# Half-wise transposes placed among matmuls, and a recurrence tail in two parts, in a two-block layer stack of split-precision matmuls

## The chip, the cores and the metric

The kernel runs on one core of one Trainium2 chip. Its time is device microseconds (us) of one execution of the whole program, the median of several runs. Engines are named as in the profile: PE is TensorE (matmuls), PEld its weight loads, DVE is VectorE, ACT is ScalarE, POOL is GpSimd, SP is SyncE, which issues nearly all DMA loads here.

## The reference, cut to what matters

There are 256 tokens of width 1024. The first block has two layers. Each normalises `x`, projects it and runs three branches: a gated MLP (a), latent attention (b) and a gated linear recurrence (c). They are projected, gated and summed:

```
h = rmsnorm(x, pre_norm_g[l]);  proj = h @ w_in[l]
y_a = gmlp_spatial(u, v, ...) * silu(z_a)
y_b = mla_attention(...)      * silu(z_b)
y_c = rg_lru(x_c, ...)        * silu(z_c)
merged = (sigmoid(g_a) * (y_a @ w_proj_a[l]) + sigmoid(g_b) * (y_b @ w_proj_b[l])
          + sigmoid(g_c) * (y_c @ w_proj_c[l]))
x = x + rmsnorm(merged @ w_out[l], post_norm_g[l])
```

`rg_lru` is a recurrence along the tokens on 1280 channels: with `a = exp(log_a)` and `b = sqrt(max(1 - a*a, 0)) * i * x`, the state is `h[t] = a[t] * h[t-1] + b[t]`. The gates `a` and `i` come from small block-diagonal products.

The second block has two layers too. Layer 0 mixes by pooling windows, layer 1 by a sparse attention (NSA). Both then do

```
x = x + conv_ffn(rmsnorm(x, norm_ffn[i]), ...)               # 1024 -> 2 x 2816 -> 1024
gate = sigmoid(rmsnorm(x, norm_ple[i]) @ ple_gate[i])
x = x + gate * (p[i] @ ple_proj[i])
```

and the attention of layer 1 starts from two norms of the `x` that this gate leaves in layer 0. A last norm gives the output. Everything is float32.

## The kernel before

**Numbers and tiles.** A float32 operand is kept as two parts of a reduced type that TensorE takes, a high part `hi` and a low part `lo`. A product is three matmuls (`mm3`, lines 481 to 483: hi by hi, hi by lo, lo by hi). The 256 tokens are two halves of 128. A token-major product has one half's features as the stationary operand and 512 weight columns moving; a feature-major one (`feat_pair`) has weights as the stationary operand and all 256 tokens moving. The results stand in PSUM tiles `psA` (four buffers) and `psB`.

**Weights.** They come in chunks of 512 KB in one fixed order (`Stream.get`, line 382). A request for a chunk first issues the loads of the next chunks (`raw_ahead`, 3) on SP's queue into four buffers `raw`, and the splits of the next ones (`split_ahead`, 2): the high part on ScalarE (L376), the low part on VectorE in two pieces of 512 columns (L379), in seven buffers `hi` and `lo`. A `raw` buffer is free again once its low part is made.

**Order.** The scheduler sets the order on each engine, from the order in which the program is written and from the data that each instruction needs. An engine then works through its own list strictly in order.

**A token-major group.** `tok_halves` asks for all four chunks of a product, then does half 0 with all of them, then half 1. `tok_group` was a list of its two results. `tok_pair` does it for two such products at once (`PAIR_HELD`, 6 of 8 chunks held).

**A norm.** `norm` returns `run(half)`. With `fold` it multiplies `x` by a row of gains (L555, tile `h`), starts the sum of squares on ScalarE (L512) and the inverse root behind it (L501, L502), and at once transposes `h` on TensorE (L538, 128 x 128 each) and splits the result into `hT` (ScalarE L488, VectorE L489; L491 and L492 where a scale is applied). The factor of the norm itself is applied later.

**The recurrence's tail** (`first_layer`, lines 975 to 1001). The merge order is `ga` 0 and `pa` 0 (the gate and the projection of branch a, first 512 columns), the recurrence's gates for its first half, `ga` 1 and `pa` 1, and the other gates (`gates`, tanh on ScalarE L967 into `tmp`, exp L973 into `av`). Then follow both groups of the merge gate `gc` with their tanh (L898) and the part that changes, in this order:

```
tg = [gate("gc", n) for n in range(2)]                                                    # L980
...
    nc.vector.tensor_tensor(tv[j], av[j], av[j], op=ALU.mult)                             # L985, five tiles
    nc.vector.tensor_scalar(tv[j], tv[j], 1.0, None, op0=ALU.min)                         # L986
    nc.scalar.activation(tv[j], tv[j], AF.Sqrt, bias=quarter, scale=-0.25)                # L987
...
    nc.vector.tensor_tensor(xc[j], xc[j], tv[j], op=ALU.mult)                             # L989, five tiles
        nc.vector.tensor_tensor_scan(ctile(av, ct), ctile(av, ct), ctile(xc, ct), 0.0, ...)   # L992, ten halves
```

Behind it the branch's own gate `zc` is computed in five feature-major pairs of tiles (240 matmuls of 256 columns). Each has a tanh (L617), a product (L618) and one with the state (L1001), and is split into `yc` (L491, L492). `pc`, the projection of `yc`, is two token-major groups of 60 matmuls. Its results are added to `merged`, which is transposed (L538) for `w_out`. In layer 1 the tile `pT` (256 KB) and a row of gains in two halves are loaded between the scans and `zc`.

**The feed-forward network** (`ffn`). It has 22 tiles of activations, and its last seven down-projections (`FFN_TAIL`) are done half 0 first, then half 1, 42 matmuls each. Behind all of them each half's sums are added to `x` (L1165) and the next norm's `run` follows. **The gate** (`ple`, lines 1182 to 1199) does the same behind `tok_pair`: for each half tanh, product and sum (L1195 to L1197), then `run`. In layer 0 this is the norm from which the attention starts; in layer 1 it is the last one, without transposes.

Of the kernel before, what the change touches and what calls it, by code (L numbers as in the profile page):

```python
# [16 lines left out]
P = 128  # L17
# [170 lines left out]
FFN_TAIL = 7  # L188
PAIR_HELD = 6
# [229 lines left out]
class Net:  # L419
# [123 lines left out]
    def norm(self, *key, dst=None, rs=None, fold=None):  # L543
# [6 lines left out]
        def run(half):  # L550
            if fold:
                hs = self.u2s("h", 2)
                for n, h in enumerate(hs):
                    cs = slice(n * 512, (n + 1) * 512)
                    self.nc.vector.tensor_tensor(h, self.x[half][:, cs], gain[n], op=ALU.mult)  # L555
            if run_rs[half] is None:
                run_rs[half] = self.rs_x(half, fold or 1.0)
            if not fold:
                hs = self.scaled_x(half, run_rs[half], gain)
            for n, h in enumerate(hs):  # L560
                self.transpose_split(h, dst, half, 4 * n, 4)

        run.dst, self.rs = dst, run_rs
# [15 lines left out]
    def tok_pair(self, key, f):  # L579

        ps = [[self.psA(), self.psA()] for _ in range(2)]
        def part(half, i, w):
            n, c = divmod(i, 4)
            for k in range(2):
                kg = 2 * c + k
                self.mm3(ps[n][half], f.pair(kg, half), (w[0][:, k, :], w[1][:, k, :]), kg == 0, kg == KD - 1)
# [146 lines left out]
    def first_layer(self, l):  # L733
# [119 lines left out]
        for n in range(2):  # L853
            ps = self.tok_group(("v", l, n), hT)
# [23 lines left out]
        for n in range(2):  # L878
            ps = self.tok_group(("u", l, n), hT)
# [4 lines left out]
        for n in range(2):  # L884
            ps = self.tok_group(("za", l, n), hT)
# [8 lines left out]
        def gate(gk, n):  # L894
            ts = []
            for ps in self.tok_halves((gk, l, n), hT):
# [4 lines left out]
        def project(pk, n, y, kts, ts, first=False):  # L901
            for half, ps in enumerate(self.tok_halves((pk, l, n), y, kts=kts)):
# [71 lines left out]

        for kind, i in MERGE_ORDER:
# [4 lines left out]
        tg = [gate("gc", n) for n in range(2)]  # L980
# [135 lines left out]
    def ffn(self, l):  # L1116
# [26 lines left out]

        def down(*js):
            ws = [self.w.get(("down", l, j), 512) for j in js]
            for half in range(2):
                sl = slice(half * P, half * P + P)
                for j, (wh, wl) in zip(js, ws):
                    f = act[j]
                    for n in range(2):  # L1150
                        self.mm3(acc[half][n], (f[:, 0, sl], f[:, 1, sl]), (wh[:, n, :], wl[:, n, :]),
                                 j == 0, j == KF - 1)
# [8 lines left out]
        down(*range(KF - FFN_TAIL, KF))  # L1161
        for half in range(2):
# [3 lines left out]
            nxt(half)  # L1166
# [8 lines left out]
    def ple_in(self, l, n):  # L1175
        if n == 0:
            self.pp = [[], []]
        ps = self.tok_group(("pp", l, n), self.pf, kts=2)
# [5 lines left out]
    def ple(self, l):  # L1184
# [5 lines left out]
        pss = self.tok_pair(("pg", l), hT)  # L1190
        for half in range(2):
            for n in range(2):
                cs = slice(n * 512, n * 512 + 512)
                t = self.tmp()
                nc.scalar.activation(t, pss[n][half], AF.Tanh, scale=rs[half])  # L1195
                nc.vector.scalar_tensor_tensor(t, t, 1.0, self.pp[half][n], op0=ALU.add, op1=ALU.mult)
                nc.vector.tensor_tensor(self.x[half][:, cs], self.x[half][:, cs], t, op=ALU.add)  # L1197
            nxt(half)
# [15 lines left out]
    def nsa(self):  # L1214
# [15 lines left out]
        ps = self.tok_group(("kv", 0), h1)  # L1230
# [72 lines left out]
        def keys_values(s):  # L1303
            ps = self.tok_group(("kv", 1 + s), h1)
# [43 lines left out]
        def queries(n):  # L1348
            ps = self.tok_group(("qb", n), hT)
# [206 lines left out]
```

## Time and profile before

| what | value |
| --- | --- |
| median of three runs | 1441.75 us (1443.41, 1441.58, 1441.75) |
| profiled execution | 1441.76 us |
| its span in the trace | 1440.0 us |
| mean granted TensorE clock | 0.994 of full speed |
| busy in the span: PE, DVE, ACT, POOL | 1399.3, 1049.4, 844.6, 92.0 us |
| DMA | 249.32 MB, mean 173 GB/s |

The span runs from the first to the last instruction on the core, and the time of an execution holds 1.76 us more around it. Busy time counts an instruction from its start to its modelled end; register work and DMA issue are not counted. PE's and PEld's times lie beside each other, so they are not added. Means over the span hide stages with different limits, and the losses spoken of below are fractions of a per cent of it.

### The profile page before, as it was taken

Reading aid. Unit: us, or ns where it says so; the run is one execution under the profiler, and the core shown is the slowest. Engines: PE = TensorE matmul, PEld = TensorE weight load, DVE = VectorE, ACT = ScalarE, POOL = GpSimd, SP = SyncE. Lnnn points to the kernel's source line nnn. Section 1 sums busy time; section 2 is a strip of 40 time slices with the busy share of each in tenths; the row PEclk is TensorE's granted clock in tenths of the full one; section 3 lists DMA queues with packets and bytes.
Section 4 is the critical chain, followed back from the end, with each engine's and each line's share of the span. In section 5 each row is a group of like instructions: output and inputs, shape, how many; then the busy total and the mean of one; then the engine's idle time right before and its main releaser. Section 6 shows DMA issues by size and latency. Waiting matters only on the chain.

```text
span 1440.0 us, 23026 instructions
## 1 busy us (share of the span) xinstructions
PE 1399.3 (97%) x8506; PEld 1236.1 (86%) x8506; DVE 1049.4 (73%) x2131; ACT 844.6 (59%) x1421; POOL 92.0 (6%) x155
## 2 busy tenths in 40 slices
PE   6999999999999999999999999999999999999997
PEld 6987889889789878898897899999888778999985
DVE  7856748659767676577687688777696788787765
ACT  6665545656455665456655466555565796665554
POOL 1000002100010000021000000000010440000000
PEclk9999999999999999999999999999999999999999
DMA  8553555564646634665656555555555115655652
GB/s 282 183 196 117 163 188 190 168 214 136 228 139 207 214 118 129 194 201 161 203 175 231 163 181 186 191 178 189 183 172 171 50 38 189 194 180 189 188 164 86
DMA packets 73408, 249.32 MB, mean 173 GB/s; under 512 B 8272, under 2 KB 8912, under 8 KB 73296
## 3 DMA queue, kind: packets, MB, share of 16 engines
q1 hardware_dynamic: 72576, 245.95, 52.1%
q10 hardware_dynamic: 720, 1.91, 0.5%
q8 instruction: 67, 1.10, 0.3%
q14 instruction: 45, 0.37, 0.1%
HBM read 246.77 MB, written 1.05 MB: 172 GB/s over the span
## 4 chain that ended last, share of the span: by engine, by line
PE 81%; DVE 9%; ACT 5%; DMA 3%; issue 2%; POOL 1%; POOLq 0%; ACTq 0%; DVEq 0%; SPq 0%
PE psA L481 22%; PE psA L483 22%; PE psA L482 22%; PE psB L481 3%; DVE lo L379 3%; PE psB L482 3%; DMA raw<-in_w_dram 3%; PE psB L483 3%; ACT hi L376 2%; PE psB L538 1%; ACT es L1415 1%; DVE av L992 1%; POOL rs L502 1%; PE psB L1054 1%; PE psB L1036 1%
## 5 line engine op out<-in xcount | busy, mean ns | idle before, releaser
L379 DVE TENSOR_TENSOR lo<-raw,hi 128x512 fp32r<-128x512 f32 (+2 forms) x897 | 585.0, 679 | 221.3 <-ACT hi L376 215.8
L376 ACT ACTIVATE hi<-raw 128x1024 fp32r<-128x1024 f32 (+3 forms) x449 | 467.6, 1045 | 309.8 <-PE psA L483 112.3
L482 PE MATMUL psA<-hT,hi 128*128 128x256 f32 x1160 | 328.6, 283 | 0.5 <-DVE hT L489 0.5
L483 PE MATMUL psA<-hT,lo 128*128 128x256 f32 x1160 | 328.2, 283 | 0.0
L481 PE MATMUL psA<-hT,hi 128*128 128x256 f32 x1160 | 328.1, 283 | 0.0
L481 PE MATMUL psA<-hi,hT 128*128 128x512 f32 (+2 forms) x592 | 230.6, 390 | 3.2 <-ACT hT L488 3.2
L482 PE MATMUL psA<-lo,hT 128*128 128x512 f32 (+2 forms) x592 | 228.5, 386 | 1.4 <-DVE lo L379 1.4
L483 PE MATMUL psA<-hi,hT 128*128 128x512 f32 (+2 forms) x592 | 229.1, 388 | 0.0
L482 PEld LDWEIGHTS psA<-hT,hi 128*128 128x128 f32 x1160 | 221.9, 191 | 2.0 <-DVE hT L489 0.7
L481 PEld LDWEIGHTS psA<-hT,hi 128*128 128x128 f32 x1160 | 221.8, 191 | 1.6 <-ACT hT L488 0.2
L483 PEld LDWEIGHTS psA<-hT,lo 128*128 128x128 f32 x1160 | 221.9, 191 | 0.0
L481 PEld LDWEIGHTS psA<-hi,hT 128*128 128x128 f32 x592 | 111.8, 189 | 22.6 <-ACT hT L488 4.1
L482 PEld LDWEIGHTS psA<-lo,hT 128*128 128x128 f32 x592 | 111.5, 188 | 21.4 <-DVE lo L379 2.1
L483 PEld LDWEIGHTS psA<-hi,hT 128*128 128x128 f32 x592 | 111.5, 188 | 20.4 <-DVE hT L489 0.5
L502 POOL TENSOR_TENSOR rs<-ms,mhalf 128x1 f32<-128x1 f32 x34 | 28.3, 832 | 977.1 <-DVE ms L501 788.1
L1135 DVE SCALAR_TENSOR_TENSOR tmp<-psA,colt,tmp 128x255 f32<-128x255 f32 (+1 forms) x176 | 84.2, 478 | 1.2
L481 PE MATMUL psB<-hi,fact 128*128 128x512 f32 x176 | 68.8, 391 | 0.0
L482 PE MATMUL psB<-lo,fact 128*128 128x512 f32 x176 | 68.8, 391 | 0.0
L483 PE MATMUL psB<-hi,fact 128*128 128x512 f32 x176 | 68.5, 389 | 0.0
L1132 ACT ACTIVATE tmp<-psA,colt 128x256 f32<-128x256 f32 x88 | 48.5, 551 | 1.9
L936 POOL CAST es<-xs 64x256 fp32r<-64x256 f32 x48 | 29.4, 640 | 270.1 <-ACT xs L488 269.3
L512 ACT ACTIVATE junk<-x 128x512 bf16<-128x512 f32 x36 | 22.6, 629 | 36.8 <-DVE x L1165 14.0
(342 smaller groups left out, 2238.1 us busy)
## 6 DMA issues: line engine op xcount, KB each, us to landing
raw<-in_w_dram SPq DMA_DIRECT2D x414, 512.0 KB, 3.6
raw<-in_w_dram SPq DMA_DIRECT2D x24, 384.0 KB, 3.8
row<-in_rows_dram SPq DMA_DIRECT2D x34, 256.0 KB, 5.4
raw<-in_w_dram SPq DMA_DIRECT2D x8, 448.0 KB, 3.2
raw<-in_w_dram SPq DMA_DIRECT2D x4, 480.0 KB, 3.3
x<-in_x_dram SPq DMA_DIRECT2D x4, 256.0 KB, 4.3
pm<-in_pm_dram ACTq DMA_DIRECT2D x2, 512.0 KB, 5.2
out_dram<-h SPq DMA_DIRECT2D x4, 256.0 KB, 2.1
```

What stands on the lines that cost most here:

```text
L376: self.nc.scalar.activation(hi[:, :n], t[:, :n], AF.Copy)
L379: self.nc.vector.tensor_tensor(lo[:, c], t[:, c], hi[:, c].bitcast(F32), op=ALU.subtract)
L481: mm(ps, a[0], b[0], start=start, stop=False)
L482: mm(ps, a[0], b[1], start=False, stop=False)
L483: mm(ps, a[1], b[0], start=False, stop=stop)
L502: nc.gpsimd.tensor_tensor(rs, ms, self.mhalf, op=ALU.pow)
L512: nc.scalar.activation(junk[:, :s.shape[1]], s, AF.Square, scale=float(n) ** -0.5 / mul, accum_out=ss[:, i:i + 1])
L538: nc.tensor.transpose(ps[:, i, :], src[:, (done + i) * P:(done + i + 1) * P], self.cf("ident"))
L936: nc.gpsimd.tensor_copy(edges[p][m][i][r], xs.pair(ct)[i][r].bitcast(F32))
L992: nc.vector.tensor_tensor_scan(ctile(av, ct), ctile(av, ct), ctile(xc, ct), 0.0, op0=ALU.mult, op1=ALU.add)
L1132: nc.scalar.activation(dst, src, AF.Identity, bias=self.col("fb", ct, l), scale=self.col("fw", 2 * 2 * KF + ct, l))
L1135: nc.vector.scalar_tensor_tensor(dst[:, s:], src[:, :S - s], self.col("fw", (2 - s) * 2 * KF + ct, l), dst[:, s:], op0=ALU.mult, op1=ALU.add)
```

## The change

The diff, cut to its core. Not shown are the other callers of `tok_group` (`v`, `u`, `za`, `pp`, `kv`, `qb`), which now call `list(self.tok_halves(...))` and so keep their old order, and `down`, whose inner loop is now a function `down_one` with the same matmuls.

```diff
+FFN_LATE = 3
+PAIR_LATE = 4
...
-        mm(ps, a[1], b[0], start=False, stop=stop)
+        return mm(ps, a[1], b[0], start=False, stop=stop).ins
...
-        def run(half):
+        hs = [None, None]
+
+        def scale(half):
             if fold:
-                hs = self.u2s("h", 2)
...
-            for n, h in enumerate(hs):
+        def turn(half):
+            for n, h in enumerate(hs[half]):
                 self.transpose_split(h, dst, half, 4 * n, 4)
...
     def tok_group(self, key, f, N=512, kts=KD, kper=2):
-        return list(self.tok_halves(key, f, N, kts, kper))
+        ps = [self.psA(), self.psA()]
+        for c in range(-(-kts // kper)):
+            wh, wl = self.w.get((*key, c), N)
+            for half in range(2):
+                for kg in range(c * kper, min(kts, (c + 1) * kper)):
+                    k = kg % kper
+                    self.mm3(ps[half][:, :N], f.pair(kg, half), (wh[:, k, :], wl[:, k, :]), kg == 0, kg == kts - 1)
+        return ps
...
-    def tok_pair(self, key, f):
+    def tok_pair(self, key, f, first=None, turn=None):
...
+        if first:
+            first(0, [ps[0][0], ps[1][0]])
         for i in range(8 - PAIR_HELD, 8):
-            part(1, i, ws[i])
+            ins = part(1, i, ws[i])
+            if turn and i == 8 - PAIR_HELD + PAIR_LATE - 1:
+                with self.tc.issue_after(ins):
+                    turn(0)
+        if first:
+            first(1, [ps[0][1], ps[1][1]])
...
-            for ps in self.tok_halves((gk, l, n), hT):
+            for ps in (self.tok_group if gk != "gb" else self.tok_halves)((gk, l, n), hT):
...
-            for half, ps in enumerate(self.tok_halves((pk, l, n), y, kts=kts)):
+            for half, ps in enumerate((self.tok_group if pk == "pa" else self.tok_halves)((pk, l, n), y, kts=kts)):
...
+        self.w.raw_ahead, self.w.split_ahead = 6, 4
         for kind, i in MERGE_ORDER:
...
-        tg = [gate("gc", n) for n in range(2)]
...
         for j in range(5):
-            nc.vector.tensor_tensor(tv[j], av[j], av[j], op=ALU.mult)
+            nc.scalar.activation(tv[j], av[j], AF.Square)
             nc.vector.tensor_scalar(tv[j], tv[j], 1.0, None, op0=ALU.min)
+        for j in range(5):
             nc.scalar.activation(tv[j], tv[j], AF.Sqrt, bias=quarter, scale=-0.25)
+        tg = [gate("gc", 0)]
         for j in range(5):
             nc.vector.tensor_tensor(xc[j], xc[j], tv[j], op=ALU.mult)
...
+        tg.append(gate("gc", 1))
+        self.w.raw_ahead, self.w.split_ahead = 3, 2
...
         nxt = self.norm("ple", l, fold=0.5)
-        down(*range(KF - FFN_TAIL, KF))
-        for half in range(2):
+
+        def residual(half):
...
-            nxt(half)
+            nxt.scale(half)
+
+        js = range(KF - FFN_TAIL, KF)
+        ws = [self.w.get(("down", l, j), 512) for j in js]
+        for half in range(2):
+            for j, w in zip(js, ws):
+                ins = down_one(j, half, w)
+                if half and j == KF - FFN_LATE:
+                    with self.tc.issue_after(ins):
+                        nxt.turn(0)
+            residual(half)
+        nxt.turn(1)
```

In words: a norm's `run` is cut into `scale` (gains, sum of squares) and `turn` (transposes and splits). `issue_after(ins)` lets nothing that is written in its block run on the engine of `ins` before `ins`. So half 0's transposes stand behind the half-1 matmuls of the feed-forward's tile 19 of 22 and, in the gate of layer 0, behind the fourth of half 1's last six chunks (`ple` passes the sums of a half as `first` and the transposes as `turn`; in layer 1 it passes no `turn`). `tok_group` now goes through the chunks in order and does both halves with each; `ga`, `pa` and `gc` use it, while `gb`, `pb` and `pc` keep half after half. The recurrence's squares are done on ScalarE (one Square for each tile), and squares, minima and roots are written ahead of both groups of `gc`, products and scans between the two. From `ga` to the end of `gc` loads are issued six chunks ahead and splits four.

How this moves instructions shows in the order on each engine. On ScalarE, in layer 0, from the recurrence's last gates (L967) to the roots, before (L376 are high parts of weight chunks, L898 the tanh of `gc`'s groups, L987 the roots):

```order
L967 ACTIVATE tmp<-psA,lrub_717 128x256 x3
L376 ACTIVATE hi<-raw 128x1024 x2
L898 ACTIVATE tmp<-psA 128x512
L376 ACTIVATE hi<-raw 128x1024 x3
L898 ACTIVATE tmp<-psA 128x512
L376 ACTIVATE hi<-raw 128x1024
L898 ACTIVATE tmp<-psA 128x512
L376 ACTIVATE hi<-raw 128x1024 x3
L898 ACTIVATE tmp<-psA 128x512
L376 ACTIVATE hi<-raw 128x1024
L987 ACT_TABLE_LOAD
L987 ACTIVATE tv<-tv,quarter 128x512 x5
```

The same place now (L378 are high parts, L1011 the squares, L1014 the roots, L924 the tanh of `gc`):

```order
L378 ACTIVATE hi<-raw 128x1024
L993 ACTIVATE tmp<-psA,lrub_717 128x256 x3
L1011 ACTIVATE tv<-av 128x512 x5
L1014 ACT_TABLE_LOAD
L1014 ACTIVATE tv<-tv,quarter 128x512 x5
L378 ACTIVATE hi<-raw 128x1024 x3
L924 ACT_TABLE_LOAD
L924 ACTIVATE tmp<-psA 128x512 x2
L378 ACTIVATE hi<-raw 128x1024 x4
L924 ACTIVATE tmp<-psA 128x512
L378 ACTIVATE hi<-raw 128x1024
L924 ACTIVATE tmp<-psA 128x512
```

Squares, table load and roots stand ahead of all four tanh of `gc` and of eight splits, where they stood behind them.

On VectorE, in the same layer, the recurrence's tail before (L379 are low parts of chunks, L985 squares, L986 minima, L989 products, L992 scans; four more scans follow):

```order
L379 TENSOR_TENSOR lo<-raw,hi 128x512 x18
L985 TENSOR_TENSOR tv<-av 128x512 x2
L986 TENSOR_SCALAR tv<-tv 128x512 x2
L985 TENSOR_TENSOR tv<-av 128x512 x2
L986 TENSOR_SCALAR tv<-tv 128x512 x2
L985 TENSOR_TENSOR tv<-av 128x512
L989 TENSOR_TENSOR xc<-xc,tv 128x512
L986 TENSOR_SCALAR tv<-tv 128x512
L992 SCALAR_TENSOR_TENSOR av<-av,xc 128x256 x2
L989 TENSOR_TENSOR xc<-xc,tv 128x512 x2
L992 SCALAR_TENSOR_TENSOR av<-av,xc 128x256 x4
L989 TENSOR_TENSOR xc<-xc,tv 128x512 x2
```

And now (L381 are low parts, L1012 minima, L1017 products, L1020 scans, L644 the first product behind a tanh of `zc`):

```order
L381 TENSOR_TENSOR lo<-raw,hi 128x512
L1012 TENSOR_SCALAR tv<-tv 128x512 x5
L1017 TENSOR_TENSOR xc<-xc,tv 128x512 x2
L1020 SCALAR_TENSOR_TENSOR av<-av,xc 128x256 x4
L1017 TENSOR_TENSOR xc<-xc,tv 128x512 x2
L381 TENSOR_TENSOR lo<-raw,hi 128x512 x6
L1020 SCALAR_TENSOR_TENSOR av<-av,xc 128x256 x4
L1017 TENSOR_TENSOR xc<-xc,tv 128x512
L381 TENSOR_TENSOR lo<-raw,hi 128x512
L1020 SCALAR_TENSOR_TENSOR av<-av,xc 128x256 x2
L381 TENSOR_TENSOR lo<-raw,hi 128x512 x16
L644 SCALAR_TENSOR_TENSOR tmp<-tmp,psA 128x512
```

The five squares are gone here, low parts stand among the scans, and sixteen of them (eight chunks) between the last scan and the first product of `zc`.

On TensorE, at the end of the feed-forward network of layer 1, before (`fact` are the activations of the last tile, half 1; L538 are the transposes of half 0's `h`; `psA_15181` is the first product of the gate behind):

```order
L481 MATMUL psB_13042<-hi_15016,fact_14937 128x512
L482 MATMUL psB_13042<-lo_15017,fact_14937 128x512
L483 MATMUL psB_13042<-hi_15016,fact_14937 128x512
L538 MATMUL psB_15134<-cft_72,h_15121 128x128 x4
L538 MATMUL psB_15141<-cft_72,h_15122 128x128 x4
L481 MATMUL psA_15181<-hi_15023,hT_14982 128x512
L482 MATMUL psA_15181<-lo_15024,hT_14982 128x512
```

And now (L540 are the same transposes; `hi_15002` is the chunk of tile 19, `hi_15009` that of tile 20):

```order
L483 MATMUL psB_13042<-hi_15002,fact_14749 128x512
L484 MATMUL psB_13042<-lo_15003,fact_14749 128x512
L485 MATMUL psB_13042<-hi_15002,fact_14749 128x512
L540 MATMUL psB_15122<-cft_72,h_15079 128x128 x4
L540 MATMUL psB_15129<-cft_72,h_15080 128x128 x4
L483 MATMUL psB_13041<-hi_15009,fact_14843 128x512
L484 MATMUL psB_13041<-lo_15010,fact_14843 128x512
```

Half 0's transposes have moved ahead of half 1's last twelve matmuls. Half 1's own stand as before behind the first matmuls of the gate's product: eight and eight of them lie ahead of its two groups of four now, seven and ten before.

## Rows read from the trace of the kernel before

**Rows 1.** The page, busy time of each engine (share of the span) and instructions.

```profile
PE 1399.3 (97%) x8506; PEld 1236.1 (86%) x8506; DVE 1049.4 (73%) x2131; ACT 844.6 (59%) x1421; POOL 92.0 (6%) x155
```

**Rows 2.** View of waits, PE: tile waited for, us in total, times, longest.

```profile
PE psA L481 <- ACT yc L491: 3.5, 3, 1.9
PE psA L481 <- ACT hT L488: 3.2, 4, 1.3
```

**Rows 3.** PE's timeline, recurrence tails: start, us, operation, count [idle before <-releaser].

```profile
327.39 0.28 PE L481 MATMUL psA<-hT,hi 128*128 128x256 f32 x1
...
356.18 0.40 PE L481 MATMUL psA<-hi,yc 128*128 128x512 f32 x1
...
361.42 0.39 PE L483 MATMUL psA<-hi,yc 128*128 128x512 f32 x1
...
363.69 0.50 PE L481 MATMUL psA<-hi,yc 128*128 128x512 f32 x1 [1.88 <-ACT yc L491]
...
387.82 0.38 PE L538 MATMUL psB<-cft,merged 128*128 128x128 f32 x2
...
756.81 0.40 PE L481 MATMUL psA<-hi,yc 128*128 128x512 f32 x1
...
788.77 0.49 PE L538 MATMUL psB<-cft,merged 128*128 128x128 f32 x3
```

**Rows 4.** Two windows of `pc`: us, PE busy (starts), granted clock, DMA share, GB/s.

```profile
365.20:369.20 4.00, 4.00 (x12) 0.57 0.93 274
373.20:377.20 4.00, 4.00 (x20) 1.00 0.91 267
```

**Rows 5.** DVE's timeline, layer 0's recurrence tail.

```profile
327.98 1.29 DVE L985 TENSOR_TENSOR tv<-av 128x512 f32<-128x512 f32 x2
...
339.17 2.43 DVE L992 TENSOR_TENSOR_SCAN av<-av,xc 128x256 f32<-128x256 f32 x4
...
342.10 0.69 DVE L379 TENSOR_TENSOR lo<-raw,hi 128x512 fp32r<-128x512 f32 x1
...
343.30 1.29 DVE L379 TENSOR_TENSOR lo<-raw,hi 128x512 fp32r<-128x512 f32 x2
```

**Rows 6.** ACT's timeline, layer 0's recurrence tail.

```profile
307.04 2.04 ACT L376 ACTIVATE hi<-raw 128x1024 fp32r<-128x1024 f32 x2
...
329.15 1.28 ACT L987 ACT_TABLE_LOAD   x1
330.45 2.57 ACT L987 ACTIVATE tv<-tv,quarter 128x512 f32<-128x512 f32 x4
...
346.12 1.06 ACT L376 ACTIVATE hi<-raw 128x1024 fp32r<-128x1024 f32 x1 [1.51 <-DMA raw<-in_w_dram]
...
360.40 0.58 ACT L617 ACTIVATE tmp<-psA 128x512 f32<-128x512 f32 x1
...
363.02 0.61 ACT L491 ACTIVATE yc<-tmp 128x512 fp32r<-128x512 f32 x1
```

**Rows 7.** Window over all engines: us, busy of each, clock, DMA share, GB/s.

```profile
336.00:342.00 6.00, 6.00 (x52) 6.00 (x51) 6.00 (x11) 1.92 (x3) 0.00 (x0) 1.00 0.00 0
```

**Rows 8.** The page, DMA issues: queue, count, KB each, us from issue to landing.

```profile
raw<-in_w_dram SPq DMA_DIRECT2D x414, 512.0 KB, 3.6
```

**Rows 9.** Timelines of DVE, ACT and PE, end of layer 1's feed-forward network.

```profile
1397.42 1.29 DVE L555 TENSOR_TENSOR h<-x,row 128x512 f32<-128x512 f32 x2
...
1406.49 1.28 DVE L1165 TENSOR_TENSOR x<-x,psB 128x512 f32<-128x512 f32 x2
...
1406.84 1.06 ACT L376 ACTIVATE hi<-raw 128x1024 fp32r<-128x1024 f32 x1 [1.59 <-DMA raw<-in_w_dram]
...
1408.43 0.50 PE L481 MATMUL psA<-hi,hT 128*128 128x512 f32 x1 [1.26 <-ACT hT L488]
```

**Rows 10.** PE's timeline, ends of layer 0's feed-forward network and gate.

```profile
1027.23 0.50 PE L481 MATMUL psA<-hi,hT 128*128 128x512 f32 x1 [0.40 <-ACT hT L488]
...
1051.54 0.50 PE L481 MATMUL psA<-hi,hT 128*128 128x512 f32 x1 [0.47 <-ACT hT L488]
```

More of the change, by code (lines that the diff above doesn't have):

```diff
@@ L548, in norm @@
         run_rs = rs or [None, None]
-        def run(half):
+        hs = [None, None]
+        def scale(half):
             if fold:
-                hs = self.u2s("h", 2)
-                for n, h in enumerate(hs):
+                hs[half] = self.u2s("h", 2)
+                for n, h in enumerate(hs[half]):
                     cs = slice(n * 512, (n + 1) * 512)
@@ L558, in run @@
             if not fold:
-                hs = self.scaled_x(half, run_rs[half], gain)
-            for n, h in enumerate(hs):
+                hs[half] = self.scaled_x(half, run_rs[half], gain)
+        def turn(half):
+            for n, h in enumerate(hs[half]):
                 self.transpose_split(h, dst, half, 4 * n, 4)
+        def run(half):
+            scale(half)
+            turn(half)
+        run.scale, run.turn = scale, turn
         run.dst, self.rs = dst, run_rs
@@ L585, in part @@
                 kg = 2 * c + k
-                self.mm3(ps[n][half], f.pair(kg, half), (w[0][:, k, :], w[1][:, k, :]), kg == 0, kg == KD - 1)
+                ins = self.mm3(ps[n][half], f.pair(kg, half), (w[0][:, k, :], w[1][:, k, :]), kg == 0, kg == KD - 1)
+            return ins
         def get(i):
@@ L853, in first_layer @@
         for n in range(2):
-            ps = self.tok_group(("v", l, n), hT)
+            ps = list(self.tok_halves(("v", l, n), hT))
             for half in range(2):
@@ L878, in first_layer @@
         for n in range(2):
-            ps = self.tok_group(("u", l, n), hT)
+            ps = list(self.tok_halves(("u", l, n), hT))
             for half in range(2):
@@ L1142, in up, with down_one @@
             act[j] = f
+        def down_one(j, half, w):
+            sl, f = slice(half * P, half * P + P), act[j]
+            for n in range(2):
+                ins = self.mm3(acc[half][n], (f[:, 0, sl], f[:, 1, sl]), (w[0][:, n, :], w[1][:, n, :]),
+                               j == 0, j == KF - 1)
+            return ins
         def down(*js):
@@ L1146, in down @@
             for half in range(2):
[L1147 to L1152, printed above, removed]
+                for j, w in zip(js, ws):
+                    down_one(j, half, w)
         for j in range(KF):
@@ L1165, in ffn @@
                 nc.vector.tensor_tensor(self.x[half][:, cs], self.x[half][:, cs], acc[half][n], op=ALU.add)
-            nxt(half)
+            nxt.scale(half)
+        js = range(KF - FFN_TAIL, KF)
+        ws = [self.w.get(("down", l, j), 512) for j in js]
+        for half in range(2):
+            for j, w in zip(js, ws):
+                ins = down_one(j, half, w)
[4 more added lines that the diff above has]
+        nxt.turn(1)
         self.hT = nxt.dst
@@ L1189, in ple, with residual @@
         nxt = self.norm("nkv", fold=1.0) if l == 0 else self.final()
-        pss = self.tok_pair(("pg", l), hT)
-        for half in range(2):
+        def residual(half, pss):
             for n in range(2):
@@ L1194, in ple @@
                 t = self.tmp()
-                nc.scalar.activation(t, pss[n][half], AF.Tanh, scale=rs[half])
+                nc.scalar.activation(t, pss[n], AF.Tanh, scale=rs[half])
                 nc.vector.scalar_tensor_tensor(t, t, 1.0, self.pp[half][n], op0=ALU.add, op1=ALU.mult)
                 nc.vector.tensor_tensor(self.x[half][:, cs], self.x[half][:, cs], t, op=ALU.add)
-            nxt(half)
+            if l == 0:
+                nxt.scale(half)
+            else:
+                nxt(half)
+        self.tok_pair(("pg", l), hT, residual, nxt.turn if l == 0 else None)
+        if l == 0:
+            nxt.turn(1)
         self.hT = nxt.dst
@@ L1229, in nsa @@
             z.append(zt)
-        ps = self.tok_group(("kv", 0), h1)
+        ps = list(self.tok_halves(("kv", 0), h1))
         kv = []
@@ L1348, in queries @@
         def queries(n):
-            ps = self.tok_group(("qb", n), hT)
+            ps = list(self.tok_halves(("qb", n), hT))
             for half in range(2):
```

6 lines of the change are left out of this document (3 added, 3 removed).

## The prediction

> **What bounds the kernel now.** The page comes first: TensorE is busy for 1399.3 of 1440.0 us [rows 1], so nothing is won except where it waits or runs slowly. The view of waits says for whom it waits inside the program: 3.5 us in three waits for `yc`, 3.2 us in four for `hT` [rows 2]. Both tiles are made by the code that changes. Third comes TensorE's timeline at the recurrence's tail [rows 3]. In layer 0 the projection `pc`, 120 matmuls of 512 columns, begins at 356.18, and the transposes of `merged` behind it at 387.82: 31.64 us. Its 24th matmul starts 5.24 us after its first, 0.228 us a step, so 120 need 27.3 us and 4.3 us are lost. In layer 1 it takes 788.77 - 756.81 = 31.96 us, 4.6 us too long. Of layer 0's loss 1.88 us is one wait for `yc`. Behind it the granted clock fell: 0.57 on average over four microseconds with 12 matmul starts, against 20 at 1.00 a little later [rows 4]. That is the lower of the two levels, 1.2 GHz, for most of the stretch, entered after the wait.
>
> Why `yc` is late is read on VectorE and ScalarE [rows 5, 6]. From 327.98 on VectorE does squares, minima, products and ten scans, and it ends its last scan at 341.6. For these 13.6 us it makes no low part of a weight chunk, so no `raw` buffer comes free, and from 336 to 342 DMA moves 0 GB/s [rows 7]. A load needs 3.6 us to land [rows 8], so ScalarE's queue then stands at its weight splits: the one at 346.12 waited 1.51 us for DMA. The tanh of the gate `zc` is queued among them. The last `zc` matmul was out at 356.18, its tanh started at 360.40, the last `yc` at 363.02, and TensorE had needed it at 361.65.
>
> **The recurrence's tail (both layers).** `zc` is 240 matmuls of 256 columns from 327.39 to 356.18, 0.12 us each; `gc` is 96 of 512, so it starts at 327.39 - 96 x 0.228 = 305.5 [rows 3]. The new order puts ScalarE's five squares, table load and five roots right behind the gates' last tanh, which ended about 307.0, where rows 6 begin. Squares go at the price of another 512-element pass, 0.58 us: done at 309.9. Table load 1.28, roots 2.57 / 4 each: done at 314.4. Three high parts follow at 1.02 us. VectorE multiplies two tiles once the first roots are there (1.3 us), scans four half tiles (2.43), multiplies two (1.3) and is at the next low part at about 317.0; at 1.29 us a chunk the second chunk of `gc`'s second half is ready at 318.3 [rows 5].
>
> TensorE asks for it later: four chunks of `gc` 0 and one of `gc` 1 are split by then (the one at ScalarE's place before its last tanh, as now), and a chunk feeds both token halves, 12 matmuls or 2.74 us. Five last until 305.5 + 13.7 = 319.2. The margin is 0.9 us. It grows behind that, since chunks come every 1.29 us while VectorE is free, and the remaining six scans (3.7 us) and a product fall between chunks that stand two or more ahead.
>
> So the long stretch without a low part is split, by my estimate, into about 8.5 us (from 308.5, when the low part of the chunk at ScalarE's place before its last tanh is done, to 317.0) and 3 us, both under `gc`, not `zc`. Five squares leave VectorE (1.29 us for two, 3.1 us in all). By 342.1, where VectorE now makes its first low part after the scans [rows 5], I count three chunks more, 3 x 2.88 = 8.6 us of `zc`. The lag of the last tanh, 360.40 - 356.18 = 4.2 us, is covered in layer 0. I take the whole 4.3 us there. In layer 1 the tile `pT` and two gain rows, 256 KB each by their shapes, are loaded in the same place, in idle time now; at 274 GB/s [rows 4] they cost 2.9 us of DMA, which leaves 5.7 us. The loss may not vanish, so I take 4.2 of 4.6 us.
>
> Both halves of `ga`, `pa` and `gc` now go chunk by chunk. A group keeps its 48 matmuls: price 0, since TensorE alternates between two accumulators and the other two PSUM buffers cover the tanh. Their cover gone, each would cost a 0.6 us pass per group, six groups a layer. The deeper raw and split distances add no transfer.
>
> **The feed-forward tails.** In layer 1 TensorE waits 1.26 us for `hT` after the transposes: ScalarE had the copy queued behind a split that itself waited 1.59 us for DMA [rows 9]. The new order puts the eight transposes of half 0 ahead of the last 12 matmuls of half 1 and the copy ahead of that split, so 2.7 us hide it. What is late next is half 1: its two sums (1.28 us) begin only when its last matmul is out, then comes a product at 0.69 us for the first tile and 0.6 more for the second. The order leaves eight matmuls, 1.8 us, ahead of its transposes; with 0.2 us to get going the first product is there after 2.2 us. TensorE waits 0.4 + 0.2 = 0.6 us. Gain 1.26 - 0.6, so 0.6. In layer 0 the present wait is 0.40 us [rows 10] against the same 0.6 us or a little less: I take 0.
>
> **The gate's tail in layer 0.** TensorE waits 0.47 us for `hT` [rows 10]. Half 0's transposes move ahead of the last 12 matmuls; its products come early enough (they need half 0 alone). Half 1's second transposes may wait for the last sum, up to 0.5 us, and the query norm's up to 0.3 us, in place of waits that 0.1 us hide now. Gain 0.5, bounds -0.3 and 1.0. The final gate in layer 1 has no transposes and stays.
>
> **Sum.** 4.3 + 4.2 + 0.6 + 0 + 0.5 = 9.6 us. The profiled execution took 1441.76 us (span 1440.0 and 1.76 around it), and the median is 1441.75. **1441.76 - 9.6 = 1432.2 us.**
>
> A rule speaks against one edit. The row shows a VectorE product at 1.29 us for two and a 512-element ScalarE pass at 0.58 us [rows 5, 6], so moving a square costs nothing by itself. The Trainium skill, "ScalarE: Activation LUTs", Rules for kernel authors, says to keep multiplications on VectorE, which it gives as up to about three times faster per element (in bf16). Were a ScalarE square twice its row, 2.9 us more would stand ahead of the roots, the 0.9 us margin would be 2.0 us short in each layer, and the time would be 1436.2 us. These tiles are f32, so I give this 0.04.
>
> **The rivals.**
> Layer 1 keeps its wait. For it: its last tanh trails more now, and its loads no longer fall in idle time. Against: three chunks of lead. It gives 1432.2 + 4.2 = 1436.4 us. With the case above and partial ones between: 0.15.
>
> The change does nothing measurable: the wait for `yc` only moves, because DMA still stops during the first 8.5 us and the late chunks then hold up `zc`'s tanh in the same way. The feed-forward gains of 1.1 us remain, 1440 to 1442 us. For it: ScalarE's queue still has the splits ahead of each tanh, and `raw` still has four buffers. Against: the stretch begins 20 us earlier and 28.8 us of `zc` follow. 0.12.
>
> Slower: ScalarE's block of 7.4 us ahead of the splits starves `gc`. It decides by how many chunks are ready when `gc` starts: five give the margin above. With two, TensorE would stop at 305.5 + 5.5 = 311.0 until 318.3, 7.3 us, and 2.1 us of lower clock, as behind `yc` now: 9.4 us a layer, 18.8, against 9.6 gained: 1451 us. With three it is 6.7 a layer and 1445.6. For it: the lead must be built up by four buffers while gates and tanh share ScalarE. Against: the kernel already has as many chunks split at that place. 0.08.
>
> More than forecast: the feed-forward and gate tails lose all their waits (2.1 us instead of 1.1) and the attention behind them starts as much earlier: 1427 to 1429.5 us. 0.07.
>
> **How the numbers follow.** My forecast, 1429.5 to 1435 us by the bounds (0.4 us a layer in the tail, 0.6 in the feed-forward, 0.8 in the gate, 1 us of shifted waits in the attention), has 0.58. No change can be told from one under 0.2%, 2.9 us. Faster by more is 0.58 + 0.15 + 0.07 = 0.80, the same 0.12, slower 0.08. The range leaves out the slower case, half of the unchanged one and half of the best: 1428 to 1441 us.
>
> **What would show it.** Right: no wait for `yc` over 0.5 us, `pc` at 27 to 28 us in both layers with the clock at 1.00, DMA moving all through `zc`, no wait inside `gc`; waits of a few tenths for `h` at half 1's transposes in place of the 1.26 us. Wrong: a wait for a `lo` tile inside `gc` or `zc`, a lower clock in either, a last tanh of `zc` still several microseconds behind its matmuls, or new waits for `tmp` and `h` in the attention's first projections.

## The result and the profile after

The changed kernel takes 1431.01 us (median of four runs, 1429.59 to 1431.35), against 1441.66 us for the kernel before on the same chip: a ratio of 0.9923, 95% interval 0.9907 to 0.9938. It was forecast at 1432.2 us. The profiled execution took 1431.35 us, its span is 1429.5 us, and the mean granted clock is 0.996. Work and transfers are the same (8506 matmuls, 249.32 MB); of VectorE's instructions ten have gone to ScalarE, the squares.

The page's busy time, and the view of waits for TensorE (tile waited for, us in total, times, longest), in the order of [rows 1, 2]:

```profile
PE 1394.7 (98%) x8506; PEld 1233.7 (86%) x8506; DVE 1044.6 (73%) x2121; ACT 848.2 (59%) x1431; POOL 91.6 (6%) x155
...
PE psA L483 <- ACT hT L490: 1.3, 1, 1.3
...
PE psB L790 <- ACT krs L490: 0.7, 1, 0.7
```

No wait for `yc` is left, and one of four for `hT`. A wait for `krs`, a small tile of the attention in the first block's second layer, does not stand in the trace of before; it is taken up below. TensorE's timeline at both tails answers to [rows 3]:

```profile
356.10 0.40 PE L483 MATMUL psA<-hi,yc 128*128 128x512 f32 x1
...
383.33 0.93 PE L540 MATMUL psB<-cft,merged 128*128 128x128 f32 x7
...
753.35 0.40 PE L483 MATMUL psA<-hi,yc 128*128 128x512 f32 x1
...
780.59 0.60 PE L540 MATMUL psB<-cft,merged 128*128 128x128 f32 x4
```

`pc` takes 383.33 - 356.10 = 27.23 us and 780.59 - 753.35 = 27.24 us. That is 120 x 0.227, the pace of the matmuls, so nothing is lost in it. The recurrence's work now lies under `gc`. ScalarE's timeline there, with the last tanh and the last `yc` behind it, answers to [rows 6]:

```profile
306.95 2.74 ACT L1011 ACTIVATE tv<-av 128x512 f32<-128x512 f32 x5
309.71 1.28 ACT L1014 ACT_TABLE_LOAD   x1
311.00 3.18 ACT L1014 ACTIVATE tv<-tv,quarter 128x512 f32<-128x512 f32 x5
314.09 2.94 ACT L378 ACTIVATE hi<-raw 128x1024 fp32r<-128x1024 f32 x3
...
356.23 1.06 ACT L378 ACTIVATE hi<-raw 128x1024 fp32r<-128x1024 f32 x1 [1.30 <-issue]
357.19 0.58 ACT L643 ACTIVATE tmp<-psA 128x512 f32<-128x512 f32 x1
359.84 0.63 ACT L493 ACTIVATE yc<-tmp 128x512 fp32r<-128x512 f32 x1 [2.08 <-DVE tmp L1031]
```

The last tanh now starts 357.19 - 356.10 = 1.1 us behind the start of `pc`, where it was 4.2. From 340 on no split ahead of it waits for DMA; the last one ahead waits 1.30 us for something that the view does not name ("issue"). VectorE's timeline of the first part of the tail, and DMA in two stretches (us, PE, PEld, DVE, ACT and POOL busy, clock, DMA share, GB/s), answer to [rows 5, 7]:

```profile
307.65 0.69 DVE L381 TENSOR_TENSOR lo<-raw,hi 128x512 fp32r<-128x512 f32 x1
...
311.76 1.30 DVE L1017 TENSOR_TENSOR xc<-xc,tv 128x512 f32<-128x512 f32 x2 [1.61 <-ACT tv L1014]
312.98 2.43 DVE L1020 TENSOR_TENSOR_SCAN av<-av,xc 128x256 f32<-128x256 f32 x4
315.33 1.27 DVE L1017 TENSOR_TENSOR xc<-xc,tv 128x512 f32<-128x512 f32 x2
316.52 3.70 DVE L381 TENSOR_TENSOR lo<-raw,hi 128x512 fp32r<-128x512 f32 x6
320.13 2.43 DVE L1020 TENSOR_TENSOR_SCAN av<-av,xc 128x256 f32<-128x256 f32 x4
...
323.06 0.68 DVE L381 TENSOR_TENSOR lo<-raw,hi 128x512 fp32r<-128x512 f32 x1
```

```profile
312.00:318.00 6.00, 6.00 (x28) 4.96 (x27) 6.00 (x11) 5.98 (x8) 0.00 (x0) 1.00 0.00 0
...
336.00:342.00 6.00, 6.00 (x52) 6.00 (x52) 5.09 (x9) 4.30 (x6) 0.00 (x0) 1.00 0.80 245
```

The stretch without a transfer is still there. It lies from 312 to 318 now, and from 336 to 342, under `zc`, DMA moves 245 GB/s where it moved nothing. VectorE makes no low part from 308.3 to 316.52, 8.2 us, and then for 2.9 us from 320.13 on (the last two scans follow one piece later), where one stretch of 13.6 us had been.

**A ledger of the difference.** Both traces have the same number of matmuls, so the start of the one with the same number in each can be compared outside the places that the change reorders. The forecast stands first, then the difference of the two traces in each stretch, then that of a second trace of the changed kernel (`after_again`, below) to the one of before, in us:

| stretch | forecast | first trace | second trace |
| --- | --- | --- | --- |
| all ahead of layer 0's `zc` | 0 | -0.09 | +0.76 |
| `zc` and `pc`, layer 0 | -4.3 | -4.38 | -4.54 |
| layer 1's first products (`hT` at 411, `krs` at 435) | 0 | +1.01 | +0.47 |
| `zc` and `pc`, layer 1 | -4.2 | -4.66 | -4.79 |
| pooling layer | 0 | 0.00 | -0.09 |
| feed-forward tail, layer 0 | 0 | -0.66 | -0.57 |
| gate's tail and first products of the attention | -0.5 | -1.47 | -1.43 |
| rest of the attention (lower clock at 1112) | 0 | +1.02 | +0.11 |
| feed-forward tail, layer 1 | -0.6 | -1.07 | -1.18 |
| sum | -9.6 | -10.30 | -11.26 |

### The profile page after: what moved, and what is told of

The parts are those of the page before. It is cut to its first block, busy times and chain, and to the rows that moved or that the text cites. A ratio compares the mean times of both kernels' runs of the same rounds, so it can differ in the third digit from the quotient of the medians.

```text
span 1429.5 us, 23022 instructions
## 1 busy us (share of the span) xinstructions
PE 1394.7 (98%) x8506; PEld 1233.7 (86%) x8506; DVE 1044.6 (73%) x2121; ACT 848.2 (59%) x1431; POOL 91.6 (6%) x155
## 2 busy tenths in 40 slices
DMA packets 73408, 249.32 MB, mean 174 GB/s; under 512 B 8272, under 2 KB 8912, under 8 KB 73296
## 4 chain that ended last, share of the span: by engine, by line
PE 88%; DVE 4%; ACT 4%; DMA 3%; issue 1%; POOL 1%; POOLq 0%; ACTq 0%; DVEq 0%; SPq 0%
PE psA L483 24%; PE psA L484 24%; PE psA L485 24%; PE psB L483 3%; PE psB L484 3%; PE psB L485 3%; DMA raw<-in_w_dram 2%; ACT hi L378 1%; DVE lo L381 1%; PE psB L540 1%; PE psB L1066 1%; POOL rs L504 1%; PE psB L1084 1%; ACT es L1466 1%; PE psA L1315 1%
## 5 line engine op out<-in xcount | busy, mean ns | idle before, releaser
L381 DVE TENSOR_TENSOR lo<-raw,hi 128x512 fp32r<-128x512 f32 (+2 forms) x897 | 586.7, 679 | 221.3 <-ACT hi L378 216.5
L378 ACT ACTIVATE hi<-raw 128x1024 fp32r<-128x1024 f32 (+3 forms) x449 | 466.4, 1043 | 309.4 <-PE psA L485 108.1
```

What stands on the lines that cost most here:

```text
L378: self.nc.scalar.activation(hi[:, :n], t[:, :n], AF.Copy)
L381: self.nc.vector.tensor_tensor(lo[:, c], t[:, c], hi[:, c].bitcast(F32), op=ALU.subtract)
```

## The experiments

Twelve kernels ran, eleven variants and the changed kernel again, four at a time on one chip, each beside the kernel before. Medians are in us; ratios are to the kernel before, with the 95% interval in brackets.

**The tail alone (`tail_only`).** The feed-forward and gate tails are put back:

```diff
-                ins = down_one(j, half, w)
-                if half and j == KF - FFN_LATE:
-                    with self.tc.issue_after(ins):
-                        nxt.turn(0)
-            residual(half)
-        nxt.turn(1)
+                down_one(j, half, w)
+        for half in range(2):
+            residual(half)
+            nxt.turn(half)
...
-        self.tok_pair(("pg", l), hT, residual, nxt.turn if l == 0 else None)
+        pss = self.tok_pair(("pg", l), hT)
```

> The kernel after with the feed-forward and gate tails put back as before, so only the recurrence's tail (and the chunk order of ga, pa, gc) is changed. My theory: the two tails are worth 4.4 and 4.7 us as the trace of after shows, and about 1 us comes back in later waits (hT at 410, krs at 435), so 8 to 9 us under the kernel before: 1432.5 to 1433.5 us. Rival (the gain is shared evenly with the transposes, or the tail only works together with them): 1436 us or more.

Measured: 1432.76 against 1442.99, 0.9933 [0.9920, 0.9946]. `pc` is 27.24 and 27.23 us. So the tail alone brings 9.7 us by the ratio, a little more than expected, and the waits for `hT` are back:

```profile
PE psA L483 <- ACT hT L490: 2.8, 4, 1.1
```

**The transposes alone (`turns_only`).** The reverse: the recurrence's part, its distances and the chunk order are put back.

> The kernel before with only the feed-forward and gate tails changed. My theory: the three waits for hT (0.40, 0.47 and 1.26 us) go and nothing takes their place, and the attention behind them gains up to 1 us: 2.1 to 3 us under the kernel before, 1438.7 to 1439.6 us. By the prediction's own terms, in which half 1's transposes wait 0.6 us in each feed-forward tail, it would be 1.1 us, 1440.6 us.

Measured: 1439.14, 0.9978 [0.9967, 0.9988], which is 3.2 us by the ratio, with an interval from 1.7 to 4.8. `yc` is late in both layers as before (3.9 us in three waits), and no wait stands at the feed-forward and gate tails. The two halves of the change add up as far as the times can tell: 9.7 + 3.2 = 12.9 us, against 11.1 together, and the intervals cover the difference.

```profile
PE psA L483 <- ACT yc L493: 3.9, 3, 2.3
```

**The old place (`place_undone`).** Only where the work stands is put back:

```diff
-        tv = self.u2s("tv", 5)
...
-        tg = [gate("gc", 0)]
+        tg = [gate("gc", n) for n in range(2)]
+        tv = self.u2s("tv", 5)
...
-        tg.append(gate("gc", 1))
```

> The kernel after with squares, roots, products and scans put back behind both groups of gc, under zc; squares stay on ScalarE, loads and splits stay six and four ahead, ga, pa and gc stay chunk by chunk. Theory (what matters is that VectorE's long stretch without a low part lies 20 us ahead of pc's need): yc is late again, pc takes 30 us or more in both layers, 3 to 4 us a layer lost, 1437 to 1439 us. Rival (the lead of four chunks by itself covers the stretch, wherever it lies): pc stays at 27.3 us and the time at 1431 to 1432 us.

Measured: 1438.14, 0.9969 [0.9958, 0.9981]. `pc` takes 31.23 and 31.85 us, 4.0 and 4.6 too long, as before the change. The waits for `yc`, and DMA in two stretches:

```profile
PE psA L483 <- ACT yc L493: 3.8, 4, 1.5
```

```profile
332.00:338.00 6.00, 6.00 (x52) 6.00 (x51) 5.97 (x11) 5.94 (x9) 0.00 (x0) 1.00 0.01 3
338.00:344.00 6.00, 6.00 (x52) 6.00 (x51) 5.96 (x11) 5.15 (x8) 0.00 (x0) 1.00 0.00 0
```

Squares on ScalarE, a lead of four chunks and chunk-by-chunk groups do nothing for `pc` as long as VectorE's scans stand under `zc`: DMA again stops for twelve microseconds there. The place is the cause. In layer 1 of this trace the granted clock stays up through all of `pc`, and 4.6 us are lost all the same, in waits alone (us, PE busy (starts), clock, DMA share, GB/s):

```profile
757.30:789.20 31.90, 28.73 (x123) 1.00 0.61 206
```

**The old distances (`ahead_3_2`).** The two lines that set `raw_ahead, split_ahead` are removed.

> The kernel after with loads three and splits two ahead everywhere, as before. Theory (the second chunk of gc 1 was ready only 1.6 us before its use with the longer lead): one chunk instead of three is split between the two groups of scans, the third chunk of gc 1 is about 0.5 to 1 us late in each layer, and pc still loses nothing: 1432 to 1433.5 us. Rival (the lead does nothing, since four raw buffers bound it anyway): 1431 us. Rival (the starved gc of the prediction): 5 us or more a layer, over 1440 us.

Measured: 1431.46, 0.9923 [0.9911, 0.9934]. By the time alone this is the changed kernel. By the trace `gc` takes 22.35 and 22.31 us where it takes 21.79, so 0.5 us is lost in each layer, in one place:

```profile
323.31 0.50 PE L484 MATMUL psA<-lo,hT 128*128 128x512 f32 x1 [0.22 <-DVE lo L381]
```

That is the third chunk of `gc` 1, as the theory said; `pc` stays at 27.23. By the trace the longer lead is worth about 1 us, which the time of this kernel can't show.

**Half after half (`halves`).** `ga`, `pa` and `gc` use `tok_halves` again.

> The kernel after with ga, pa and gc done half after half again, the rest as it is. Theory (chunk by chunk matters for gc 1 alone, because its low parts come 1.2 us apart behind the first scans and were ready 1.6 us ahead of use): half 0 of gc 1 now asks for a chunk every 1.36 us instead of 2.72, the second and third chunk have 0.2 to 0.4 us of margin, so gc is 21.8 to 22.5 us long and the time 1431 to 1432.5 us; pc stays 27.2 us. Rival (the order of the chunks carries the gain): gc or pc loses 2 us or more in each layer, 1435 us.

Measured: 1430.19, 0.9915 [0.9901, 0.9929]. `gc` takes 21.79 and `pc` 27.23 us in both layers, and no wait inside `gc` is over 0.2 us. The order of the chunks costs and brings nothing that shows here.

**The squares on VectorE (`squares_vector`).**

```diff
-            nc.scalar.activation(tv[j], av[j], AF.Square)
+            nc.vector.tensor_tensor(tv[j], av[j], av[j], op=ALU.mult)
```

> The kernel after with the five squares back on VectorE, in the new place. Theory (VectorE waited 1.6 us there for the first root anyway, so the engine of the squares is worth nothing; the place is): no wait in gc or zc, pc 27.2 us, 1430.5 to 1431.5 us. Rival (the 3.1 us that leave VectorE are part of the gain): low parts in gc 1 are late by 1.5 us or more in each layer, 1434 us or more.

Measured: 1431.05, 0.9918 [0.9902, 0.9933]; `gc` 21.79, `pc` 27.23 us. The engine of the squares is worth nothing in the new place. VectorE does them from 307.90 on, in the time in which the changed kernel waits for the first root, and three chunks are split ahead of the scans instead of behind four of them:

```profile
307.90 1.29 DVE L1011 TENSOR_TENSOR tv<-av 128x512 f32<-128x512 f32 x2
...
313.19 3.69 DVE L381 TENSOR_TENSOR lo<-raw,hi 128x512 fp32r<-128x512 f32 x6
316.80 1.29 DVE L1017 TENSOR_TENSOR xc<-xc,tv 128x512 f32<-128x512 f32 x2
```

**The squares twice (`squares_twice`).** Each square is computed twice into the same tile.

> The kernel after with every square computed twice on ScalarE, to double the price that the prediction weighed: 2.7 us more ahead of the roots. Theory (the first low part behind the scans had 1.6 us of margin): TensorE waits 0.6 to 1.2 us for it in gc 1 of each layer and then runs on, 1432.2 to 1433.5 us if the clock stays up, up to 1436.5 us if the lower clock follows the wait in both layers. By the prediction's margin of 0.9 us, 2.0 us are lost in each layer: 1435 us. Rival (the block on ScalarE has slack elsewhere): 1431 us.

Measured: 1433.20, 0.9936 [0.9922, 0.9949]. `gc` takes 22.80 and 22.79 us, 1.0 us more in each layer, in one wait, and the clock does not fall there:

```profile
320.43 3.67 DVE L381 TENSOR_TENSOR lo<-raw,hi 128x512 fp32r<-128x512 f32 x6
...
321.15 0.50 PE L484 MATMUL psA<-lo,hT 128*128 128x512 f32 x1 [0.68 <-DVE lo L381]
```

The first low part came 320.43 - 316.52 = 3.9 us later (0.94 of it because the whole program ran that much later). Not all of that is the squares: in layer 0 the scheduler also set six scans ahead of this low part, where the changed kernel has four. Either way 3.0 us of delay cost 1.0: the first piece of the second chunk's low part had about 2 us of margin.

**Scans behind both groups (`scans_behind`).** Products and scans are written behind `gate("gc", 1)`, squares and roots stay.

> The kernel after with products and scans written behind both groups of gc, not between them; squares and roots stay ahead of gc. Theory (the scheduler sets eight of the ten scans at the same place anyway, and only the last two move behind eight more low parts): pc 27.2 us, no wait over 0.3 us in gc and zc, 1430.5 to 1431.5 us. Rival (the division of the scans carries the gain): low parts late in zc or yc late, 2 us or more in each layer, 1435 us.

Measured: 1429.61 against 1440.40, 0.9926 [0.9914, 0.9938]; `gc` 21.79, `pc` 27.23 us. What counts is where squares and roots are written; the scheduler then puts eight of the ten scans early by itself. A kernel with early roots and all scans under `zc` did not run, so the roots' place and the scans' place are not separated. No variant that ran is measurably faster than the changed kernel.

**Late transposes (`transposes_late`).** `FFN_LATE` is 1 and `PAIR_LATE` 6, so half 0's transposes follow half 1's last matmul.

> The kernel after with half 0's transposes held behind the last of half 1's matmuls, in both feed-forward tails and in the gate, so that only the sums and gains stay early. Theory (the copy to hT must stand ahead of the split that waits for DMA): the waits for hT return, 0.4, 0.5 and about 1 us, so 1.5 to 2.2 us over after: 1432.5 to 1433.2 us. Rival (the early products alone made the difference): 1431 us, no wait for hT over 0.2 us.

Measured: 1432.95, 0.9949 [0.9935, 0.9962], against 1430.15 for the changed kernel on the same chip: 2.8 us, somewhat more than the three waits that return, 0.25, 0.47 and 1.61 us (a wait costs more than its idle time, as shown below). So the place of the transposes removes them, and the early sums by themselves do not. The view of waits, and the last of the three in TensorE's timeline:

```profile
PE psA L483 <- ACT hT L490: 3.0, 4, 1.6
```

```profile
1400.44 0.50 PE L483 MATMUL psA<-hi,hT 128*128 128x512 f32 x1 [1.61 <-ACT hT L490]
```

**A second look (`after_again`).** The changed kernel, unchanged.

> The changed kernel unchanged, for a second look on the same chip. Theory: 1431 us, pc 27.2 us in both layers; the waits for krs at 435 (0.70 us) and the lower clock at 1112, which the first trace has, belong to single executions and need not return. Rival (they belong to the change): both return.

Measured: 1430.15 against 1440.40, 0.9926 [0.9914, 0.9938]. The lower clock at 1112 is gone. The wait for `krs` is there again, 0.43 us. Of the other kernels some have it there (0.66 in `tail_only`, 0.77 in `squares_vector`), others do not (`halves`, `squares_twice`, `place_undone`). In the first trace the copy is queued on ScalarE behind a split that waited 0.63 us for its chunk. Why that chunk lands late in some executions stays open, and so does whether the change brings this wait: nine of the thirteen traces of changed kernels have it, and the one trace of before has not.

**Two attempts at more.** In the pooling layer TensorE waits 2.7 us at 812 for a normalised tile. `pool_order` holds the second half's pooling matmuls behind the first half's mixing matmuls (`with self.tc.issue_after(mixed(0)): pooled(1, 1)`). `pp_early` moves the second group of `pp` ahead of the pooling, in the code and in the weight stream.

> The kernel after with one more edit of the same kind in the pooling layer: the second half's pooling matmuls are held behind the first half's mixing matmuls, which TensorE could do during its 2.7 us wait for the second half's normalised tile at 812. Theory (the wait is a matter of order, and so is the lower clock behind it): the wait falls under 0.5 us and 2.5 to 3.7 us are won, 1427 to 1429 us. Rival (the norm behind the mixing is a chain of its own length, so the wait moves to the transposes at 827): 1430.5 to 1431.5 us.

> The kernel after with the second of the two groups of p @ ple_proj (12 matmuls, 2.7 us) done together with the first, ahead of the pooling matmuls; its weight chunk moves in the stream to the same place. Theory (TensorE's 2.7 us wait at 812 is time in which this group can be done, and the lower clock comes behind such a wait): the wait falls under 0.5 us, TensorE works on at 814.7 as before, and what follows is shorter by the missing group where TensorE bounds it and by the lower clock, 1.5 to 2.5 us in all: 1428.5 to 1429.5 us. Rival (what follows is the chain of the second half's norm, so its transposes wait longer instead): within 0.5 us of after, 1430.5 to 1431.5 us.

Measured: `pool_order` 1434.27, 0.9943 [0.9930, 0.9957]; `pp_early` 1432.92, 0.9945 [0.9932, 0.9957]. On the same chips the changed kernel and the variants equal to it stand at 0.9915 to 0.9926, so both are slower, and both theories fell, as did the rivals' times. TensorE's timelines:

```profile
815.74 0.39 PE L485 MATMUL psA<-hi,uf 128*128 128x256 f32 x1 [3.97 <-DVE uf L491]
```

```profile
830.92 1.41 PE L541 MATMUL psB<-cft,tmp 128*128 128x128 f32 x6 [3.93 <-DVE tmp L529]
```

In `pool_order` the matmuls that should fill the wait need the low part of `uf`, which VectorE has queued behind the norm's chain, so TensorE waits 3.97 us for that. In `pp_early` the rival had the place right and the price wrong: TensorE is ahead at 816 and then waits 3.93 us for the second half's norm: what follows is a chain of sums, norm and transposes that the moved matmuls had been covering.

## Why the prediction came out

**The place of the loss was right.** VectorE's stretch without a low part stops DMA, the late chunks hold ScalarE's queue, the tanh behind them is late, and `yc` with it. `place_undone` shows it: with everything else of the tail changed, 4.0 and 4.6 us are lost again. By 342.1 I had counted three chunks more split than before; it is four (229 pieces of low parts against 221).

**The two tails** were taken at 4.3 and 4.2 us and brought 4.4 and 4.7. In layer 1 I held back 0.4 us for loads that no longer fall into idle time; they cost nothing.

**The margin in `gc`** was put at 0.9 us: low part at 317.0, second chunk at 318.3, need at 319.2. It is 316.52 in the trace, ready at 317.8, needed at 319.4: 1.6 us. A square is 2.74 / 5 = 0.55 us, not 0.58, and the roots end at 314.2, not 314.4. The rest of the half microsecond is that I added whole durations on VectorE, where the next instruction starts before the last one ends: the steps from 311.76 are 1.22, 2.35 and 1.19 us, not 1.3, 2.43 and 1.3. With the squares doubled the loss was 1.0 us a layer, where my margin would have given 2.0. So the case of a square at twice its row was a real risk, at half the price of 4 us that I gave it. The slower rival, `gc` starved with two or three chunks ready, did not come: no wait over 0.1 us lies in `gc` of the changed kernel.

**The rule that was weighed.** Squares cost 0.55 us each on ScalarE here and 0.64 on VectorE (1.29 for two), f32 tiles of 512 elements. The Trainium skill, "ScalarE: Activation LUTs", Rules for kernel authors, prefers VectorE for multiplications, with up to about three times its speed in bf16 for operations with one source. For these f32 tiles the trace shows no such difference, and `squares_vector` shows that the choice does not move the time.

**The feed-forward tails were under-sized**: 0.6 us in layer 1 and 0 in layer 0 forecast, 1.1 and 0.7 measured. Two terms of the sum were wrong.

One is what a wait is worth. I took the idle times of the view, 1.26 and 0.40 us. Such a time counts from the modelled end of the instruction before, when the next could already have started, and the matmul behind the wait then takes 0.34 us to the next where 0.23 is the pace. In layer 1, before and after:

```profile
1408.43 0.50 PE L481 MATMUL psA<-hi,hT 128*128 128x512 f32 x1 [1.26 <-ACT hT L488]
1408.77 0.39 PE L482 MATMUL psA<-lo,hT 128*128 128x512 f32 x1
```

```profile
1397.81 0.39 PE L483 MATMUL psA<-hi,hT 128*128 128x512 f32 x1
1398.03 0.39 PE L484 MATMUL psA<-lo,hT 128*128 128x512 f32 x1
```

The second of these matmuls starts 10.74 us earlier now; ahead of the tail it was 9.23. So the wait had cost 1.5 us, and the one of layer 0, measured the same way, 0.7.

The other is the 0.6 us wait that I gave half 1's transposes, "0.4 + 0.2". VectorE and TensorE there, in layer 1 and then in layer 0:

```profile
1396.70 1.28 DVE L491 TENSOR_TENSOR hT<-psB,hT 128x512 fp32r<-128x512 f32 x2
1397.90 1.28 DVE L1198 TENSOR_TENSOR x<-x,psB 128x512 f32<-128x512 f32 x2
1399.09 1.29 DVE L559 TENSOR_TENSOR h<-x,row 128x512 f32<-128x512 f32 x2
```

```profile
1399.39 0.39 PE L484 MATMUL psA<-lo,hT 128*128 128x512 f32 x1
1399.92 1.23 PE L540 MATMUL psB<-cft,h 128*128 128x128 f32 x8
```

```profile
1018.14 1.31 DVE L1198 TENSOR_TENSOR x<-x,psB 128x512 f32<-128x512 f32 x2
```

```profile
1018.34 0.39 PE L485 MATMUL psB<-hi,fact 128*128 128x512 f32 x1
...
1020.15 0.40 PE L484 MATMUL psA<-lo,hT 128*128 128x512 f32 x1
1020.38 1.05 PE L540 MATMUL psB<-cft,h 128*128 128x128 f32 x8
```

In layer 0 the transposes start 0.23 us behind the matmul ahead of them, the pace, so nothing is lost. In layer 1 it is 0.53, so 0.3 us are lost, 0.4 with the slower step behind. The failing step of this term is that the two sums "begin only when its last matmul is out": the first sum needs only the first 512 columns. In layer 0 it starts at 1018.14, ahead of the last matmul at 1018.34. In layer 1 it starts when VectorE is done with the low parts of half 0's `hT`, at 1397.90. From there on the chain was also shorter than I had it: the first product is done at 1399.09 + 0.69 = 1399.8, 2.0 us behind the gate's first matmul at 1397.81 and not 2.2, and the transposes follow in 0.14, not 0.2.

**The gate** brought 1.5 us with the attention's first products, against 0.5. The wait of 0.47 us of idle time went as said, but it too was worth more, 1.0 us from start to start over the matmul that waited and the four behind it. The remaining 0.4 came in the attention's products, 0.3 of it around the transposes of `kd`, for which TensorE waits 0.24 us at 1086.00 in the kernel before and not now. I had expected such waits to grow, not to go.

**What came back.** The sum gave nothing for waits elsewhere (the bounds had 1 us for the attention). The first trace has 1.0 us more in layer 1's first products and 1.0 us of lower clock in the attention, and the second trace 0.5 and 0.1. In the first trace the terms above brought 2.6 us more than forecast, and 1.9 came back there. That these nearly cancel is why 1432.2 lies so near 1431.0, and it is luck; the 27.23 us of `pc` in both layers are not.

**The rivals.** That the change does nothing fell with the length of `pc`, that layer 1 keeps its wait with 27.24 us there. Part of "more than forecast" came true: the feed-forward and gate tails and the attention behind them gave 3.2 us in the first trace instead of 1.1, while the time stayed above that rival's 1427 to 1429.5 us.

## What to carry to other kernels

An engine that is far from full can still bound the one that is: look for the longest stretch in which VectorE (or whoever frees the load buffers) does one block of other work, see what DMA does in it, and put that block where the most split weights stand ahead. Place transposes behind matmuls that don't need them, so that the copy stands ahead of a split that may wait for its transfer. Price a wait from start to start of the matmuls around it: its idle time in the view was 0.2 to 0.6 us too little here. Before filling a wait with other matmuls, ask what those matmuls cover now and whether their operands' copies are queued behind the chain that makes the wait.

## What the runs showed of the hardware

The lower clock did not follow the waits alone. The same wait in the pooling layer, 2.7 us, was followed by the lower level (0.50 in the windows) in the first trace of the changed kernel and not in `scans_behind`, whose orders there are the same. Of the twelve traces without an edit in that layer, eight have the lower level behind this wait and four do not. The windows behind the wait in these two (us, PE busy (starts), clock, DMA share, GB/s), the first also with the stretch at 1112, which no wait over 0.1 us precedes from 832 on:

```profile
815.00:818.00 3.00, 3.00 (x16) 0.50 0.85 241
1108.70:1111.70 3.00, 2.91 (x27) 1.00 0.00 0
1111.70:1115.10 3.40, 3.40 (x10) 0.50 0.00 0
```

```profile
815.50:818.50 3.00, 3.00 (x27) 1.00 0.91 267
```

From the end of TensorE's work ahead of the wait to its next long wait it is 827.37 - 811.97 = 15.4 us in `after_again`, which has the lower clock there, and 826.50 - 812.60 = 13.9 us in `scans_behind`: 1.5 us for one such stretch. Four other traces (`place_undone`, `squares_twice`, `squares_vector`, `pp_early`) have the lower level at the place of 1112 too, while the second trace of the changed kernel has not, so it differs between executions of one kernel. How much of the spread between runs of one kernel comes from this was not separated.
